# A Mamba mixer in a two-layer trunk: its operand normalized ahead of the transposes, its decay masked by an addition, its convolution read from PSUM

## The chip, the cores and the metric

The kernel runs on one core of a Trainium2 chip. The metric is the device time of one execution in microseconds. A core has five engines with queues of their own: TensorE (PE in the profile; PEld is its weight load), VectorE (DVE), ScalarE (ACT), GpSimd (POOL) and SyncE (SP), which here issues most of the DMAs. Matmuls write to PSUM; all else lies in SBUF or DRAM.

## What is computed

A trunk of two layers on 256 tokens of width 1024, all in 32-bit floats. Each layer is a half-step feed-forward block, a token mixer, an attention into 256 memory tokens, and a second half-step block; each reads an RMS-normalized operand. Layer 0's mixer is a differential attention, layer 1's a Mamba-2 mixer (SSD), which is the part that is changed. Cut to its core:

```python
def rmsnorm(x, w):
    return x * lax.rsqrt(jnp.mean(x * x, axis=-1, keepdims=True) + EPS) * w

# the mixer: u = rmsnorm(h) @ w_in, cut into z (2048), xBC (4096), dt (32)
# xBC = silu(causal_depthwise_conv(xBC, conv_w, conv_b)), cut into x, B, C; 8 groups of 4 heads
# dt = softplus(dt + dt_bias); a = -exp(A_log) * dt; chunks of 128 tokens
a_cs = jnp.cumsum(a, axis=2)
seg = a_cs[..., :, None] - a_cs[..., None, :]
decay = jnp.exp(jnp.where(tril, seg, -jnp.inf))
cb = jnp.einsum("bclgn,bcsgn->bgcls", Cm, Bm)
y_diag = jnp.einsum("bgcls,bgrcls,bcsgrp->bclgrp", cb, decay, x)
# y = y_diag + what the state of the first chunk adds to the second + D_skip * x
# out = rmsnorm by group (y * silu(z)) @ w_out
```

The square root of the mean square is taken by token, so a token's scale can be applied to h ahead of the projection, or to the projection's result behind it. Both are used below.

## The kernel before

**Products.** PE's inputs are split into a rounded high half and the rest (`whi`/`wlo` of a weight, `xh`/`xl` of the operand), and each product is three matmuls (L209 to L211, `mm3`). A weight arrives by a DMA on SP's queue into one of four buffers; a granule of 1024 columns of it is split by a cast on ACT (L180, `whi`) and a subtraction on DVE (L181, `wlo`), two granules ahead of its use (`AHEAD = 2`), into one of four pairs of buffers. For the z projection the subtraction is put on POOL by `eng=nc.gpsimd`; it comes out there for four granules.

**Order.** The program is written by a small pipeline, `Pipe`: `pipe.after(us, f)` puts a piece of work off until PE's estimated time has advanced by `us`, with the delays in the table `T`. A scheduler then settles the order on each engine by a model of its own. Each engine executes its queue in order, so that what stands behind a waiting instruction waits too.

**The mixer** (`ssd`) runs from 800 to 1058 us of the profiled execution, in this order: `zdt` (the first 256 columns of z and the 32 of dt: 48 matmuls), the memory keys `mk` of the layer's later attention, which need nothing of the mixer (four projections in two units, 192 matmuls of 128x256), then four cycles of two groups each: the projections `b`, `c`, `xs` and z, and among them the inner work of the two groups before; then the output product.

- *Operand.* `Norm.turn` transposes h as it is (`xt`, L327) and splits it into `xh`, `xl`. `Norm.square` squares h by token on ACT, and `rpow` gets the scale `rcol` by a power on POOL (L290). As x isn't normalized, the scale is applied behind each product: to dt and z as a scalar by token, and for the convolution, which has tokens along its free dimension, by a row `rr` (`to_row`, L293: two matmuls and a copy on ACT).
- *dt.* `dt_fin` makes dt and a (`av`) with a chain of small operations on DVE and one exponential on ACT (L878 to 899). `sums` (L902) makes the cumulative sums by matmuls, `acs` by token and `acst` by head, writes `acst` to a DRAM scratch `scr` and spreads it from there with partition broadcasts: `E[g, c]`, 128x512 for each of 8 groups and 2 chunks. Four groups are spread at once, the other four later, one by one.
- *Decay.* For each group `decay` takes on POOL the decay to the chunk's end (`dte`, L928, with an exponential on ACT at L930) and E − acs (L933). `decay2` takes the minimum with 0 on DVE (L939) and the exponential on ACT (L940).
- *Convolution.* `conv` scales the projection in PSUM by the row into an SBUF tile `raw` (DVE, L945), and for each of two halves multiplies by the last tap on ACT (L950), adds three taps on DVE (L953) and applies Silu with the bias on ACT (L955). Silu and the exponential lie in different tables of ACT; a change of table shows as `ACT_TABLE_LOAD`.
- *Groups.* `cross` makes C·B (`pcb`, L1009), masks it by the triangle `triu` into `cbm` (DVE, L1011) and multiplies both chunks' E by it (DVE, L1014). `turn_x` transposes x (`tx`, L1020) and makes the products with dt, dte and D on POOL (L1026 to 1030). `inner` makes `pst` and `py`, `state` makes `pof`, adds, multiplies by Silu of z on POOL (L1059), squares on ACT, takes the scale `yrc` on POOL (L290) and applies it on DVE (L1066). `turn_y` transposes y (`ty`, L1073) and splits it for the output product.

```python
            for c in (0, 2):
                proj("a", a["xa_w_kv"][self.l], c * 256, 512, self, "mk", [fin(c), fin(c + 1)])
```

Of the kernel before, what the change touches and what calls it, by code (L numbers as in the profile page):

```python
# [15 lines left out]
P = 128  # L16
S = 256
# [9 lines left out]
         xprobs=5.0, xtp=5.5, xo=3.0, sums=9.5, cross=10.0, cross0=14.5, tx=10.0, tx0=12.0, inner=7.0, state=4.5,  # L27
         ty=9.0, e0=8.0, e1=1.0, e4=33.0, e5=16.5, e6=11.0, dec=2.2)
# [30 lines left out]
def trunk(ctx, tc, a, out):  # L59
# [153 lines left out]
    def proj(kind, src, c0, ncol, norm, name, fins, eng=None):  # L213
# [79 lines left out]
    def to_row(col, dst):  # L293

        ps = small_ps("rrow")
        for t in range(2):
            nc.tensor.matmul(ps[:, t * P:(t + 1) * P], lhsT=col[:, t:t + 1].broadcast_to([P, P]), rhs=ident,
                             start=t == 0, stop=t == 1)
        nc.scalar.copy(dst, ps[:, :S])

    class Norm:
# [3 lines left out]
        def __init__(self, gcol):  # L305
            self.g = gcol
            self.x = []
            self.ss = sm.tile([P, 16], F32, name="nss", tag="nss")
            self.n = 0

        def square(self, c):
# [23 lines left out]
        def add(self, c):  # L335

            def go():
                self.turn(c)
                self.square(c)
            pipe.after(T["turn"], go)  # L340

        def row(self):
            self.rr = sm.tile([P, S], F32, name="rrow", tag="rrow", bufs=2)
            to_row(self.col, self.rr)

    def bc2(row):
        return row.unsqueeze(1).broadcast_to([P, 2, S])
# [380 lines left out]
    class MemKV:  # L728
# [17 lines left out]
        def k_units(self, then=None):  # L746
# [10 lines left out]
            for c in (0, 2):  # L757
# [81 lines left out]
    def ssd(norm, nxt, kv):  # L839
# [8 lines left out]
        dte = const.tile([P, 32], F32, name="dte")  # L848
        E = {}
# [4 lines left out]
        def z0_dt_unit():  # L854
            w, w2 = W(w_in, 0, KT, 0, 256), W(w_in, 0, KT, 6144, 32)

            def run(*gr):
# [10 lines left out]
                def then():  # L868
                    dt_fin([p[:, 256:288] for p in ps])
                    zs0 = v2(slot("zs"))  # L870
                    for t in range(2):
                        nc.scalar.activation(zs0[:, t, :], ps[t][:, 0:256], AF.Copy, scale=norm.col[:, t:t + 1])
                    held.append(zs0)
                pipe.after(T["gate"], then)
                pipe.after(T["gate"] + 2.0, norm.row)
            units.append(([Gran(k, n, (w, 0, 256), (w2, 0, 32)) for k, n in ((0, 3), (3, 3), (6, 2))], run))

        def dt_fin(pd):  # L878
            xd = const.tile(d32, F32, name="dtx")
            for t in range(2):  # L880
                v.scalar_tensor_tensor(xd[:, t, :], pd[t], norm.col[:, t:t + 1], dtb, op0=ALU.mult, op1=ALU.add)
# [20 lines left out]
        def sums():  # L902

# [22 lines left out]
        def decay(g):  # L926
# [4 lines left out]
            for c in range(2):  # L931
                e = E[g, c]
                nc.gpsimd.tensor_tensor(e, e, acs[:, c, hs].unsqueeze(2).broadcast_to([P, 4, P]), op=ALU.subtract)  # L933
# [317 lines left out]
```

## Time and profile before

| | us |
|---|---|
| runs, median of 3 | 1337.58 (1336.15 to 1338.41) |
| profiled execution | 1336.94 |
| its span | 1335.1 |
| layer 1's mixer in it | 800.1 to 1058.0 |

The span reaches from the first to the last instruction that the profiler recorded; the execution's own time is 1.8 us longer. An engine's busy time leaves out the time in which it waits or only issues DMAs. In the rows of a window stand its bounds and length, the busy time of each engine with its number of instructions, then the clock that was granted to TensorE (1.00 is full), the DMA engines' share and GB/s. In a timeline a row is a start, a duration, the engine, the line and what it writes and reads, with the idle time ahead of it and what ended that in brackets. The slices of the page (40 equal parts, tenths of busy time) show the mixer as the stretch from the 25th slice on where DVE is fullest and POOL works at all:

```profile
DVE  5555457876566555555556456998988675655553
POOL 1000002200000000000000001444423000000000
```

### The profile page before, as it was taken

To read this page: it belongs to the slowest core of one execution; us is meant where nothing else is said; L and a number is where in the kernel's file an instruction comes from. 1 tells how busy PE (TensorE), PEld (TensorE's weight loads), DVE (VectorE), ACT (ScalarE), POOL (GpSimd) and SP (SyncE) were. 2 spreads that over 40 slices of the span, in tenths; PEclk is the share of its full clock that TensorE was granted. 3 is DMA by queue.
4 is the path that set the end of the run, shared out by engine and by line. 5 is a ranking of instruction groups with operands and counts; after the bars stand their busy time and mean duration, and the time that the engine had idled before them with its cause. 6 is when DMAs were issued, how large, how long until landed. Compare 5 with 4: busy or idle time off the path is not lost.

```text
span 1335.1 us, 17775 instructions
## 1 busy us (share of the span) xinstructions
PE 1301.0 (97%) x6991; PEld 1115.8 (84%) x6991; DVE 842.7 (63%) x1207; ACT 714.2 (53%) x1125; POOL 115.0 (9%) x109
## 2 busy tenths in 40 slices
PE   6999999999999999999999999988999999999997
PEld 5888888778988888888888889988897898888886
DVE  5555457876566555555556456998988675655553
ACT  5445544676455544444445445767756564644432
POOL 1000002200000000000000001444423000000000
PEclk9999999999999999999999999999999999999999
DMA  8564555334535554655555546634544544555551
GB/s 268 191 218 155 195 203 177 126 130 152 190 128 177 173 194 133 221 193 201 189 187 175 191 149 231 225 118 135 169 145 156 177 158 151 193 177 174 204 174 48
DMA packets 133254, 232.01 MB, mean 174 GB/s; under 512 B 5273, under 2 KB 32066, under 8 KB 133170
## 3 DMA queue, kind: packets, MB, share of 16 engines
q1 hardware_dynamic: 132496, 229.56, 52.2%
q0 software_dynamic: 368, 0.98, 0.3%
q8 instruction: 55, 0.90, 0.3%
q10 hardware_dynamic: 306, 0.33, 0.1%
q14 instruction: 29, 0.24, 0.1%
HBM read 229.77 MB, written 1.08 MB: 173 GB/s over the span
## 4 chain that ended last, share of the span: by engine, by line
PE 85%; DVE 9%; ACT 2%; POOL 2%; DMA 1%; issue 1%; POOLq 0%; DVEq 0%; ACTq 0%; SPq 0%
PE out L211 7%; PE out L210 7%; PE out L209 7%; PE gate L210 6%; PE gate L211 6%; PE gate L209 5%; PE up L209 5%; PE up L210 5%; PE up L211 5%; DVE wlo L181 2%; PE fin L209 1%; PE fin L211 1%; PE fin L210 1%; PE htp L551 1%; DVE xs L953 1%; PE mv L209 1%
## 5 line engine op out<-in xcount | busy, mean ns | idle before, releaser
L181 DVE TENSOR_TENSOR wlo<-w,whi 128x1024 fp32r<-128x1024 f32 (+1 forms) x440 | 522.9, 1194 | 408.6 <-ACT whi L180 407.6
L180 ACT CAST whi<-w 128x1024 fp32r<-128x1024 f32 (+1 forms) x444 | 446.8, 1012 | 461.4 <-PE out L211 142.5
L210 PE MATMUL gate<-wlo,xh 128*128 128x512 f32 x320 | 126.1, 394 | 2.2 <-DVE wlo L181 2.2
L209 PE MATMUL gate<-whi,xh 128*128 128x512 f32 x320 | 127.6, 400 | 0.0
L211 PE MATMUL gate<-whi,xl 128*128 128x512 f32 x320 | 125.8, 393 | 0.0
L209 PE MATMUL up<-whi,xh 128*128 128x512 f32 x320 | 124.6, 389 | 0.0
L211 PE MATMUL up<-whi,xl 128*128 128x512 f32 x320 | 124.6, 389 | 0.0
L210 PE MATMUL up<-wlo,xh 128*128 128x512 f32 x320 | 124.6, 389 | 0.0
L209 PE MATMUL out<-whi,hid_hi 128*128 128x512 f32 x264 | 103.6, 393 | 0.0
L211 PE MATMUL out<-whi,hid_lo 128*128 128x512 f32 x264 | 102.9, 390 | 0.0
L210 PE MATMUL out<-wlo,hid_hi 128*128 128x512 f32 x264 | 102.8, 390 | 0.0
L210 PEld LDWEIGHTS gate<-wlo,xh 128*128 128x128 f32 x320 | 60.9, 190 | 14.9 <-DVE wlo L181 3.0
L211 PEld LDWEIGHTS gate<-whi,xl 128*128 128x128 f32 x320 | 60.8, 190 | 12.6
L209 PEld LDWEIGHTS gate<-whi,xh 128*128 128x128 f32 x320 | 60.9, 191 | 12.0
L209 PEld LDWEIGHTS up<-whi,xh 128*128 128x128 f32 x320 | 60.1, 188 | 12.4
L211 PEld LDWEIGHTS up<-whi,xl 128*128 128x128 f32 x320 | 60.1, 188 | 12.4
L210 PEld LDWEIGHTS up<-wlo,xh 128*128 128x128 f32 x320 | 60.1, 188 | 12.4
L290 POOL TENSOR_TENSOR rcol<-msq,neghalf 128x2 f32<-128x2 f32 x8 | 5.6, 700 | 700.4 <-DVE msq L288 700.4
L211 PEld LDWEIGHTS out<-whi,hid_lo 128*128 128x128 f32 x264 | 49.6, 188 | 10.4
L210 PEld LDWEIGHTS out<-wlo,hid_hi 128*128 128x128 f32 x264 | 49.6, 188 | 10.0
L209 PEld LDWEIGHTS out<-whi,hid_hi 128*128 128x128 f32 x264 | 49.6, 188 | 10.0
L209 PE MATMUL fin<-whi,hid_hi 128*128 128x512 f32 (+1 forms) x110 | 38.3, 348 | 0.0
(352 smaller groups left out, 2777.9 us busy)
## 6 DMA issues: line engine op xcount, KB each, us to landing
w<-in_ffn_w_up_dram SPq DMA_DIRECT2D x40, 1024.0 KB, 5.0
w<-in_ffn_w_down_dram SPq DMA_DIRECT2D x40, 1024.0 KB, 5.1
w<-in_ffn_w_gate_dram SPq DMA_DIRECT2D x38, 1024.0 KB, 5.0
w<-in_ssd_w_in_dram SPq DMA_DIRECT2D x24, 1024.0 KB, 5.2
w<-in_xa_w_kv_dram SPq DMA_DIRECT2D x16, 1024.0 KB, 4.9
w<-in_da_w_in_dram SPq DMA_DIRECT2D x12, 1024.0 KB, 5.0
w<-in_xa_w_q_dram SPq DMA_DIRECT2D x8, 1024.0 KB, 5.0
w<-in_xa_w_o_dram SPq DMA_DIRECT2D x8, 1024.0 KB, 5.0
```

What stands on the lines that cost most here:

```text
L180: nc.scalar.copy(hv, src)
L181: self.eng.tensor_tensor(self.lo[:, :, o:o + n], src, hv.bitcast(F32), op=ALU.subtract)
L209: nc.tensor.matmul(o, lhsT=lh, rhs=rh, start=start, stop=False)
L210: nc.tensor.matmul(o, lhsT=lh, rhs=rl, start=False, stop=False)
L211: nc.tensor.matmul(o, lhsT=ll, rhs=rh, start=False, stop=stop)
L290: nc.gpsimd.tensor_tensor(c[:, :n], m[:, :n], neghalf[:, :n], op=ALU.pow)
L551: nc.tensor.transpose(tp[:, j, t * P:(t + 1) * P], us[t][:, (i + j) * P:(i + j + 1) * P], ident)
L953: v.scalar_tensor_tensor(o[:, j, d:], raw[:, j, :S - d], tap(k), o[:, j, d:], op0=ALU.mult, op1=ALU.add)
```

## The change

The norm ahead of layer 1's mixer is made with `first=True`: it squares h first, and when the scale is there ACT writes four tiles `hn` = h × scale, from which the transposes are made. The operand is thus normalized, the row `rr` is gone, and z, dt and the convolution use their products as they are. The key unit is cut in two: one unit of two projections ahead of `zdt`, one behind it. What followed `zdt` after a delay (`gate`) now follows at once.

The mask is a tile `later` (0 where the row may see the column, −1e30 where not), made once in `sums`. POOL adds it behind E − acs; the minimum and the triangle are gone, and E is multiplied by `pcb` in PSUM directly. The convolution reads its taps from PSUM. The scaling of y goes from DVE to ACT, and z's low halves from POOL to DVE. The delays in `T` are new.

```diff
 T = dict(gate=5.5, hid=3.0, turn=1.3, row=5.0, rot=5.5, probs=(1.0, 4.0, 7.0, 10.0), tp=6.0, heads=3.0, otp=5.0,
-         xprobs=5.0, xtp=5.5, xo=3.0, sums=9.5, cross=10.0, cross0=14.5, tx=10.0, tx0=12.0, inner=7.0, state=4.5,
-         ty=9.0, e0=8.0, e1=1.0, e4=33.0, e5=16.5, e6=11.0, dec=2.2)
+         xprobs=5.0, xtp=5.5, xo=3.0, sums=7.0, cross=9.0, cross0=13.0, tx=9.0, tx0=11.0, inner=8.0, state=6.0,
+         ty=13.0, e0=8.0, e1=5.0, e4=33.0, e5=16.5, e6=11.0, dec=6.5, first=7.0)
...
-                        xh, xl = norm.x[kt]
+                        xh, xl = pipe.need(norm.x, kt)
...
                 self.col = rpow(s[:, 0:2], 1.0 / D, 2, "rcol")
+                if self.first:
+                    self.src = [[slot("hn") for _ in range(2)] for _ in range(2)]
+                    for i in range(2):
+                        for t in range(2):
+                            nc.scalar.activation(self.src[t][i], h[t][i], AF.Copy, scale=self.col[:, t:t + 1])
+                        pipe.after(T["first"] + 1.5 * i, lambda i=i: self.turn(i))
...
-                        nc.tensor.transpose(ps[:, j, t * P:(t + 1) * P], h[t][c][:, f:f + P], ident)
+                        nc.tensor.transpose(ps[:, j, t * P:(t + 1) * P], self.src[t][c][:, f:f + P], ident)
...
-                        nc.scalar.activation(zs0[:, t, :], ps[t][:, 0:256], AF.Copy, scale=norm.col[:, t:t + 1])
+                        nc.scalar.copy(zs0[:, t, :], ps[t][:, 0:256])
                     held.append(zs0)
-                pipe.after(T["gate"], then)
-                pipe.after(T["gate"] + 2.0, norm.row)
+                then()
...
-                v.scalar_tensor_tensor(xd[:, t, :], pd[t], norm.col[:, t:t + 1], dtb, op0=ALU.mult, op1=ALU.add)
+                v.tensor_tensor(xd[:, t, :], pd[t], dtb, op=ALU.add)
...
         def sums():
+            v.tensor_scalar(later, triu, 1e30, 1e30, op0=ALU.mult, op1=ALU.subtract)
...
                 nc.gpsimd.tensor_tensor(e, e, acs[:, c, hs].unsqueeze(2).broadcast_to([P, 4, P]), op=ALU.subtract)
+                nc.gpsimd.tensor_tensor(e, e, later.unsqueeze(1).broadcast_to([P, 4, P]), op=ALU.add)
             pipe.after(T["dec"], lambda: decay2(g))

         def decay2(g):
             for c in range(2):
-                e = E[g, c]
-                v.tensor_scalar(e, e, 0.0, None, op0=ALU.min)
-                nc.scalar.activation(e, e, AF.Exp)
+                nc.scalar.activation(E[g, c], E[g, c], AF.Exp)

         def conv(ps, ch, name):
-            raw = v2(work("raw"))
-            v.tensor_tensor(raw, ps, bc2(norm.rr), op=ALU.mult)
...
-                nc.scalar.activation(o[:, j, :], raw[:, j, :], AF.Copy, scale=tap(3))
+                nc.scalar.activation(o[:, j, :], ps[:, j, :], AF.Copy, scale=tap(3))
                 for k in (2, 1, 0):
                     d = 3 - k
-                    v.scalar_tensor_tensor(o[:, j, d:], raw[:, j, :S - d], tap(k), o[:, j, d:],
+                    v.scalar_tensor_tensor(o[:, j, d:], ps[:, j, :S - d], tap(k), o[:, j, d:],
                                            op0=ALU.mult, op1=ALU.add)
...
-                    nc.scalar.activation(zs[:, t, :], ps[t], AF.Silu, scale=norm.col[:, t:t + 1])
+                    nc.scalar.activation(zs[:, t, :], ps[t], AF.Silu)
...
-                cbm = work("cbm", S).rearrange("p (c l) -> p c l", c=2)
-                v.tensor_tensor(cbm, pcb[:, 0:2, :], triu.unsqueeze(1).broadcast_to([P, 2, P]), op=ALU.mult)
-                s["cbm"] = cbm
                 for c in range(2):
-                    v.tensor_tensor(E[g, c], E[g, c], cbm[:, c, :].unsqueeze(1).broadcast_to([P, 4, P]), op=ALU.mult)
+                    v.tensor_tensor(E[g, c], E[g, c], pcb[:, c, :].unsqueeze(1).broadcast_to([P, 4, P]), op=ALU.mult)
+                s["cbm"] = True
...
-                    v.tensor_scalar(y[:, t, :], y[:, t, :], rc[:, t:t + 1], None, op0=ALU.mult)
+                    nc.scalar.activation(y[:, t, :], y[:, t, :], AF.Copy, scale=rc[:, t:t + 1])
...
+        kv.k_units(cs=(0,))
         z0_dt_unit()
-        kv.k_units()
+        kv.k_units(cs=(2,))
...
-                proj("b", w_in, 256, 256, norm, "z", [lambda ps, f=fz[1]: f([ps[:, t, :] for t in range(2)])], eng=nc.gpsimd)
+                proj("b", w_in, 256, 256, norm, "z", [lambda ps, f=fz[1]: f([ps[:, t, :] for t in range(2)])])
...
-    nx = Norm(gains("mix_norm", l))
+    nx = Norm(gains("mix_norm", l), first=l == 1)
```

How the order of the engines' work changes is shown at three places. On PE, the sums' products among the memory keys (a row is a line, an operation, what it writes and reads, and its shape), before:

```order
L210 MATMUL mk<-ml,whi 128x256
L211 MATMUL mk<-mh,wlo 128x256
L905 MATMUL acs<-av,cst 128x64
L908 MATMUL acst<-cst,av 32x128 x2
L209 MATMUL mk<-mh,whi 128x256
```

and with the change:

```order
L209 MATMUL mk<-mh,whi 128x256
L210 MATMUL mk<-ml,whi 128x256
L902 MATMUL acs<-av,cst 128x64
L905 MATMUL acst<-cst,av 32x128 x2
L211 MATMUL mk<-mh,wlo 128x256
```

Before, 132 key matmuls lie between zdt and these rows, and 60 between them and b; now 77 and 19. The 96 others are ahead of zdt, with the transposes from `hn` among them: 72 ahead of the first eight, 12 between these and the second eight, 12 behind.

On POOL, the decay of the third and fourth group (the number of an E tells its tile, two for each group). Before:

```order
L928 TENSOR_TENSOR dte_130<-E_6995,acs_128 128x4
L933 TENSOR_TENSOR E_6995<-E_6995,acs_128 128x512
L933 TENSOR_TENSOR E_6997<-E_6997,acs_128 128x512
L928 TENSOR_TENSOR dte_130<-E_6999,acs_128 128x4
L933 TENSOR_TENSOR E_6999<-E_6999,acs_128 128x512
```

and with the change, where the fourth group's dte is the last row:

```order
L925 TENSOR_TENSOR dte_130<-E_7033,acs_128 128x4
L930 TENSOR_TENSOR E_7033<-E_7033,acs_128 128x512
L930 TENSOR_TENSOR E_7035<-E_7035,acs_128 128x512
L931 TENSOR_TENSOR E_7033<-E_7033,later_131 128x512
L931 TENSOR_TENSOR E_7035<-E_7035,later_131 128x512
L925 TENSOR_TENSOR dte_130<-E_7037,acs_128 128x4
```

Twelve large operations now lie ahead of the fourth dte, where there were six.

On ACT, the exponentials of the third and fourth group, around the convolutions of b and c in the first cycle. Before (whi_7213 and whi_7257 are granules of the weights of xs):

```order
L940 ACTIVATE E_6999<-E_6999 128x512
L940 ACTIVATE E_7001<-E_7001 128x512
L950 ACTIVATE b_7167<-raw_7165,cols2_115 128x256 x2
L180 CAST whi_7213<-w_7215 128x1024
L180 CAST whi_7257<-w_7181 128x1024
L955 ACT_TABLE_LOAD
```

and with the change (whi_7274 is the second granule of the second xs projection):

```order
L927 ACTIVATE dte_130<-dte_130 128x4
L936 ACTIVATE E_7033<-E_7033 128x512
L936 ACTIVATE E_7035<-E_7035 128x512
L949 ACT_TABLE_LOAD
L949 ACTIVATE b_7148<-b_7148,cols1_114 128x256
L944 ACTIVATE b_7148<-b_7083,cols2_115 128x256
L944 ACTIVATE c_7228<-c_7159,cols2_115 128x256
L180 CAST whi_7274<-w_7192 128x1024
L180 CAST whi_7317<-w_7319 128x1024
L936 ACT_TABLE_LOAD
L936 ACTIVATE E_7037<-E_7037 128x512
L949 ACT_TABLE_LOAD
```

The first of these rows is the exponential of the fourth group's dte. The casts whi_7274 and whi_7317 stand behind it, and behind a table load, and the two halves of a convolution are apart, with loads of tables between Silu and the exponentials.

More of the change, by code (lines that the diff above doesn't have):

```diff
@@ L291, in rpow, with __init__ @@
         return c
[L293 to L299, printed above, removed]
     class Norm:
-        def __init__(self, gcol):
+        def __init__(self, gcol, first=False):
             self.g = gcol
+            self.first = first
+            self.src = h
             self.x = []
@@ L337, in go @@
             def go():
-                self.turn(c)
+                if not self.first:
+                    self.turn(c)
                 self.square(c)
             pipe.after(T["turn"], go)
[L342 to L347, printed above, removed]
     def v2(t, j=2):
@@ L744, in prep, with k_units @@
                 self.x.append((xh, xl))
-        def k_units(self, then=None):
+        def k_units(self, then=None, cs=(0, 2)):
             def fin(c):
@@ L756, in fin @@
                 return run
-            for c in (0, 2):
+            for c in cs:
                 proj("a", a["xa_w_kv"][self.l], c * 256, 512, self, "mk", [fin(c), fin(c + 1)])
@@ L848, in ssd @@
         dte = const.tile([P, 32], F32, name="dte")
+        later = const.tile([P, P], F32, name="later")
         E = {}
@@ L1090, in ssd @@
             if i == 0:
-                proj("b", w_in, 256, 256, norm, "z", [lambda ps, f=fz[1]: f([ps[:, t, :] for t in range(2)])], eng=nc.gpsimd)
+                proj("b", w_in, 256, 256, norm, "z", [lambda ps, f=fz[1]: f([ps[:, t, :] for t in range(2)])])
             else:
                 wide([(w_in, 512 * i, 512)], norm, "z",
-                     lambda ps, fz=fz: [f([p[:, j * 256:(j + 1) * 256] for p in ps]) for j, f in enumerate(fz)], eng=nc.gpsimd)
+                     lambda ps, fz=fz: [f([p[:, j * 256:(j + 1) * 256] for p in ps]) for j, f in enumerate(fz)])
         out_b(a["ssd_w_out"][0], 16, yt, upd(1.0, nxt), both=True)
```

## The prediction

> **What bounds the kernel now.** I read the page's table of engines first, then the windows of layer 1's mixer, then what TensorE (PE) waited for there, then the timelines of the engines it waited for, and the order in which each engine now issues its work.
>
> ```profile
> span 1335.1 us, 17775 instructions
> PE 1301.0 (97%) x6991; PEld 1115.8 (84%) x6991; DVE 842.7 (63%) x1207; ACT 714.2 (53%) x1125; POOL 115.0 (9%) x109
> ```
>
> PE is busy 97% of the span, so only two things can change the time: matmuls that go or come, and PE's waits. The change touches layer 1's mixer alone. Its stages, by windows (length, then busy time of PE, PEld, DVE, ACT, POOL, granted clock, DMA):
>
> ```profile
> 800.10:832.00 31.90, 31.87 (x260) 31.37 (x259) 20.60 (x39) 18.81 (x29) 1.66 (x3) 1.00 0.66 225
> 832.00:862.90 30.90, 29.80 (x247) 29.40 (x246) 27.74 (x40) 22.20 (x38) 12.40 (x12) 1.00 0.70 223
> 862.90:913.50 50.60, 45.91 (x322) 42.94 (x321) 47.65 (x77) 36.47 (x66) 22.50 (x18) 0.93 0.46 146
> 913.50:962.80 49.30, 43.42 (x308) 39.83 (x307) 43.51 (x66) 37.02 (x65) 22.50 (x20) 1.00 0.45 143
> 962.80:1006.30 43.50, 42.81 (x307) 39.80 (x306) 38.20 (x61) 25.58 (x51) 14.73 (x11) 1.00 0.43 146
> 1006.30:1058.00 51.70, 51.20 (x250) 42.70 (x249) 36.67 (x50) 29.77 (x53) 8.21 (x7) 1.00 0.49 163
> ```
>
> The rows are: dt and memory keys, the four cycles (b, c, xs, z), and the output product. Length less PE's busy time is 0.0, 1.1, 4.7, 5.9, 0.7 and 0.5 us. DVE is busy 88 to 94% of each cycle, so in the second and third PE waits for work that stands behind others on DVE:
>
> ```profile
> PE ty L1073 <- DVE y L1066: 4.7, 1, 4.7
> PE pof L1054 <- ACT state L1040: 3.1, 1, 3.1
> PE tx L1020 <- ACT xs L955: 1.4, 2, 1.0
> PE z L210 <- DVE wlo L181: 1.4, 1, 1.4
> PE xs L211 <- DVE wlo L181: 1.1, 2, 0.7
> ```
>
> The 4.7 us wait costs twice. In the five microseconds behind it the granted clock was 0.53, so about 2.3 us of work were lost there too:
>
> ```profile
> 897.00:902.00 5.00, 4.67 (x17) 4.07 (x18) 4.41 (x12) 3.06 (x9) 0.99 (x2) 0.53 0.42 118
> ```
>
> **All that the change can win** is thus 12.9 us of idle time, 2.3 us of slow clock, and small holes between matmuls, about 2 us by the records' spacing (an estimate): 17 us, of which 1.6 lie in the first cycle, 7.3 in the second, 7.3 in the third and the rest behind.
>
> **The change, part by part.** First what DVE sheds, from its groups in the mixer:
>
> ```profile
> L1014 DVE TENSOR_TENSOR E<-E,cbm 128x512 f32<-128x512 f32 x16 | 15.8, 1018 | 0.1
> L939 DVE TENSOR_SCALAR E<-E 128x512 f32<-128x512 f32 x16 | 14.2, 927 | 6.5 <-POOL E L933 6.5
> L1066 DVE TENSOR_SCALAR y<-y,yrc 128x256 f32<-128x256 f32 x16 | 6.7, 461 | 5.0 <-POOL yrc L290 5.0
> L1011 DVE TENSOR_TENSOR cbm<-pcb,cst 128x256 f32<-128x256 f32 x8 | 3.3, 410 | 0.0
> L945 DVE TENSOR_TENSOR raw<-xs,rrow 128x512 f32<-128x512 f32 x8 | 5.4, 678 | 0.0
> L181 POOL TENSOR_TENSOR wlo<-w,whi 128x1024 fp32r<-128x1024 f32 x4 | 9.6, 2405 | 33.4 <-ACT whi L180 33.4
> ```
>
> The minimum goes (14.2), the triangle (3.3), the normalization of the convolutions' inputs (16 × 0.678 = 10.8) and the scaling of y (6.7): 35.0 us. Four low halves of z's weights come back from POOL: 4 × 1.2 = 4.9. Two groups should get quicker, because of what they share with POOL. Operations between two SBUF tiles have a long tail, those with an operand in PSUM have none:
>
> ```profile
> L953 DVE SCALAR_TENSOR_TENSOR xs<-raw,cols,xs x48: 466/473/2002, 855.7 to 1003.8; 128x255 f32<-128x255 f32 x16, 128x254 f32<-128x254 f32 x16, 128x253 f32<-128x253 f32 x16
> L945 DVE TENSOR_TENSOR raw<-xs,rrow x8: 673/676/683, 854.4 to 999.4; 128x512 f32<-128x512 f32 x8
> L283 DVE SCALAR_TENSOR_TENSOR y_lo<-ty,cols,y_hi x16: 468/475/485, 904.9 to 1037.9; 128x256 fp32r<-128x256 f32 x16
> ```
>
> (shortest, median, longest, ns). The 96 taps would take their median, about 5 us less in all; the 16 multiplications of E by PSUM 0.68 in place of 1.018, 5.4 less. Together DVE sheds some 40 of its 214 us. A tap from PSUM I price as a tap from SBUF: y_lo, which reads PSUM in the same form, takes 475 against 473 ns. The Trainium skill speaks against this part: "VectorE: DVE Perf Modes", section "Rules for kernel authors", says to copy out of PSUM first where many operations follow. By that advice the removed raw copy would pay for itself; y_lo's row here says that there is nothing to be won by it, and the sum is the same without this sentence.
>
> ACT gets 16 scalings of y, priced as its squares of y (0.41, 6.6 us), and four of h, priced as its squares of h (0.62, 2.5), loses the row's copy (0.4), and by its new order has 26 table loads in the mixer where it had 16:
>
> ```profile
> L1063 ACT ACTIVATE junk<-y 128x256 f32<-128x256 f32 x16 | 6.5, 409 | 8.6 <-POOL y L1059 8.6
> L314 ACT ACTIVATE sq<-h 128x512 f32<-128x512 f32 x6 | 3.7, 620 | 0.0
> L955 ACT ACT_TABLE_LOAD x7 | 9.0, 1283 | 10.6 <-DVE xs L953 5.3 <-DVE b L953 3.8 <-DVE c L953 1.4
> ```
>
> Ten more of 1.283 us are 12.8. ACT so goes from 36.5 and 37.0 in the second and third cycle (four or three loads and four scalings more each) to about 43, against 43 to 46 of PE work: no longer a free engine. The skill's "ScalarE: Activation LUTs", section on what a table load costs, puts a switch at 2.66 us, with a drain; by that the ten would cost 26.6 us. The trace has the next operation 1.29 us behind a load's start (846.62, then 847.91), so 1.283 stands.
>
> ```profile
> L933 POOL TENSOR_TENSOR E<-E,acs 128x512 f32<-128x512 f32 x16 | 18.5, 1176 | 0.6
> L290 POOL TENSOR_TENSOR rcol<-msq,neghalf 128x2 f32<-128x2 f32 x2 | 1.4, 696 | 217.5 <-DVE msq L288 217.5
> L358 DVE SCALAR_TENSOR_TENSOR h<-out,h 128x512 f32<-128x512 f32 x2 | 1.4, 690 | 0.6 <-PE out L211 0.6
> ```
>
> POOL gets 16 additions of the mask as large as its subtractions, which take 1.18 us on average and 1.04 undisturbed (the pair at 840.13, below): 16.6 to 18.9 more, less the 9.6 above.
>
> PE loses the row's two products, under half a microsecond. The normalization now stands between the end of the last out product and the transposes. From the last matmul that is h's update (0.69 twice), the squares, the sums, the power on POOL (0.70) and four scalings, in all about 6 us; 72 key matmuls (8.7 us at the 0.12 us of the second window's 247 in 29.80) lie over it. I cost it at nothing; without the cover it would be those 6 us.
>
> **The new wait.** The keys that cover the normalization no longer cover what follows dt. From dtx to av it takes 9.85 us, then the sums, a trip through DRAM and the spread to E:
>
> ```profile
> 808.20 0.41 DVE L881 SCALAR_TENSOR_TENSOR dtx<-zdt,rcol,vec 128x32 f32<-128x32 f32 x2
> 817.83 0.23 DVE L899 SCALAR_TENSOR_TENSOR av<-dt,nega 128x64 f32<-128x64 f32 x1
> 823.86 0.33 PE L905 MATMUL acs<-av,cst 128*128 128x64 f32 x2
> 830.96 0.62 POOL L928 TENSOR_TENSOR dte<-E,acs 128x4 f32<-128x4 f32 x1 [27.16 <-DMA E<-scr]
> 836.63 3.08 POOL L933 TENSOR_TENSOR E<-E,acs 128x512 f32<-128x512 f32 x2
> 840.13 2.09 POOL L933 TENSOR_TENSOR E<-E,acs 128x512 f32<-128x512 f32 x2
> 840.20 1.66 ACT L940 ACTIVATE E<-E 128x512 f32<-128x512 f32 x3
> 844.55 1.99 ACT L180 CAST whi<-w 128x1024 fp32r<-128x1024 f32 x2
> 846.62 1.28 ACT L955 ACT_TABLE_LOAD   x1
> 847.91 0.91 ACT L955 ACTIVATE b<-b,cols 128x256 f32<-128x256 f32 x2
> ```
>
> I count from the first zdt matmul. The 48 of zdt end at 6.4 (0.133 each), the acs product follows 77 key matmuls later, at 15.6; av is there at 16.5, a wait of **0.9 us**. From acs to POOL's start it takes 7.1 us: about 24, where b's matmuls, begun at 19.5, are just ending; before, POOL began one microsecond ahead of b. Ahead of its fourth dte POOL now has twelve operations of 1.04 and three small ones, 14.1 us: that dte ends at 38.3, or up to 41.4 with three weight splits of DVE beside it (one cost POOL 1.0 us at 836.63).
>
> On ACT's new order stand behind this dte two exponentials, a table load, a Silu and two taps, and only then the cast whi of the second xs product's second part: 0.2 + 1.2 + 1.3 + 0.5 + 1.0 + 1.0 = 5.2 us, done at 43.5 to 46.6. PE wants it at about 39.7, then its wlo, behind DVE's taps. **PE waits 5 to 8 us, say 6.7.** ACT goes on late, with two more pairs of loads before it reaches the last Silu of xs, which the tx transposes need: another 2 to 5 us, say 3.6. With 0.9 us of old holes that is 11.2 in the first cycle against 1.6: **+9.6**; and behind a wait of over 4.7 us I expect the slow clock again, **+1.6**, less than the 2.3 above as 256-wide matmuls follow.
>
> In the later cycles DVE's relief does what it should, but an exponential that waits for POOL's mask additions (some 3 to 4 us) and the scaling of y behind POOL's power now hold up ACT. I leave 4.0 of 7.3 in the second (−3.3), 3.9 of 7.3 in the third (−3.4), and −1.0 behind. Start: 0.9 − 0.4 = +0.5. Sum: 0.5 + 9.6 + 1.6 − 3.3 − 3.4 − 1.0 = +4.0. The profiled run took 1336.94 us for a span of 1335.1, 0.6 under the runs' median of 1337.58: **1341.0**.
>
> **The rivals.**
> - *DVE's relief decides, faster (0.35).* ACT's place in the order harms nobody if POOL's fourth dte is done by about 33: subtractions at less than 1.04 or E landing earlier. Then the first cycle keeps its 1.6, or loses 2: 0.5 + 0.4 − 3.3 − 3.4 − 1.0 = −6.8, 1330; if the waits of the second and third cycle go wholly, 7 us more, 1323. For it: PE's two longest waits stood behind DVE. Against it: POOL's undisturbed 1.04.
> - *The two cancel (0.20).* A first-cycle wait of 7 to 8 us in all gives 1336 to 1339.
> - *ACT becomes the bound (within the slower cases, 0.13).* If ACT's 97 to 100% of PE's time in the middle cycles leaves no room, nothing is won there, and each of the 10 loads on the path is up to 1.28: +11.7 of the first terms and start, with −1 behind, and 0 to 4 of loads: 1348 to 1352.
> - *The keys don't cover the normalization:* another 2 to 4 us on any of these, if the whi casts of the keys go ahead of the squares on ACT. POOL's and DVE's share of that chain is short; I give it no chance of its own.
> - *PSUM held longer by taps:* conv's banks are wanted again 10 us or more behind their last reader by the order; dismissed.
>
> **How the numbers follow.** The likeliest, the wait for the fourth dte, has 0.32 with 1341 (1338.5 to 1347); ACT as the bound 0.13; cancelled 0.20; faster 0.35. A measurement of this kernel tells about 0.2%, 2.7 us, from no change. Faster 0.35, same 0.20, slower 0.45. The range, with the low end inside the faster case and the high end at ACT's: 1324 to 1350.
>
> **What would show it.** A PE wait of 5 us or more in the second xs product for wlo or whi, at some 40 us from the first zdt matmul; POOL's fourth dte ending at 38 or later; 26 table loads in the mixer; no wait at zdt; DVE's groups of taps at 473 ns without a tail. A fourth dte at 33, or the cast ahead of it in time, would make me wrong towards faster; ACT over 45 us busy in the middle cycles towards slower.

## The result, and the profile after

The changed kernel takes **1344.96 us** (median of 4 runs, 1343.45 to 1346.02), the kernel before 1337.99 in the same series: a ratio of 1.0053, 95% interval 1.0041 to 1.0065. It is slower by 7.0 us, on the side that was forecast and inside the range (1324 to 1350), 4 us above the number.

The page of the changed kernel, its span and its engines:

```profile
span 1341.7 us, 17757 instructions
PE 1300.8 (97%) x6987; PEld 1116.7 (83%) x6987; DVE 810.5 (60%) x1156; ACT 734.2 (55%) x1154; POOL 123.7 (9%) x121
```

PE's busy time over the whole span is the same to 0.2 us, so the span is longer by waiting: in the mixer's windows PE stood 19.2 us, where it stood 12.9 before. DVE's busy time fell by 32 us, ACT's rose by 20, POOL's by 9. The windows of the changed kernel, in the columns of those of before, with bounds at the same places of the program:

```profile
798.60:831.10 32.50, 32.19 (x263) 31.75 (x262) 21.49 (x46) 24.54 (x41) 0.70 (x1) 1.00 0.65 217
831.10:872.20 41.10, 33.07 (x252) 32.58 (x251) 20.63 (x31) 26.47 (x42) 20.67 (x20) 0.88 0.52 163
872.20:924.20 52.00, 44.24 (x316) 40.56 (x315) 39.48 (x60) 40.72 (x72) 27.00 (x23) 1.00 0.46 143
924.20:971.00 46.80, 43.69 (x304) 40.57 (x303) 34.98 (x53) 39.70 (x69) 23.78 (x20) 0.96 0.49 157
971.00:1013.70 42.70, 42.70 (x310) 40.05 (x309) 34.89 (x53) 30.43 (x60) 11.07 (x11) 1.00 0.45 155
1013.70:1064.60 50.90, 50.90 (x250) 42.82 (x250) 31.90 (x43) 29.21 (x54) 7.47 (x7) 1.00 0.48 160
```

From first b matmul to first b matmul the cycles take 41.1, 52.0, 46.8 and 42.7 us where they took 30.9, 50.6, 49.3 and 43.6: +10.2, +1.4, −2.5, −0.9; the output product wins 0.8. Counted from the last matmul of the `out` product ahead of the mixer (799.85 before, 798.35 now), b starts 0.7 us later. That is 8.1 us in the mixer. The spans differ by 6.6 alone, as the part ahead of the mixer ended 1.5 us earlier in this execution; over all profiled executions here it ended between 798.35 and 802.40. The slow clock is there too, 0.88 in the first cycle: 0.50 and 0.54 in the two stretches of 5 us from 856.1 to 866.1, behind the wait in xs. What PE waited for in the mixer, after the change:

```profile
PE xs L209 <- ACT whi L180: 6.5, 1, 6.5
PE pcb L1003 <- ACT c L949: 6.3, 3, 3.5
PE tx L1012 <- ACT xs L949: 2.9, 1, 2.9
PE z L209 <- DVE E L1005: 1.6, 1, 1.6
PE xs L211 <- DVE wlo L181: 1.5, 1, 1.5
```

The old waits for DVE's y and ACT's state are gone. In their place stands first the cast in the second xs product. Rows of POOL's timeline of the changed kernel show how late it starts (the first group's dte), then the third group and the fourth group's dte:

```profile
836.72 0.20 POOL L925 TENSOR_TENSOR dte<-E,acs 128x4 f32<-128x4 f32 x1 [34.43 <-DMA E<-scr]
848.25 0.20 POOL L925 TENSOR_TENSOR dte<-E,acs 128x4 f32<-128x4 f32 x1
848.53 2.04 POOL L930 TENSOR_TENSOR E<-E,acs 128x512 f32<-128x512 f32 x2
850.53 2.51 POOL L931 TENSOR_TENSOR E<-E,later 128x512 f32<-128x512 f32 x2
852.99 0.20 POOL L925 TENSOR_TENSOR dte<-E,acs 128x4 f32<-128x4 f32 x1
```

and ACT's, behind it:

```profile
853.23 0.20 ACT L927 ACTIVATE dte<-dte 128x4 f32<-128x4 f32 x1 [3.49 <-POOL dte L925]
853.34 1.13 ACT L936 ACTIVATE E<-E 128x512 f32<-128x512 f32 x2
854.47 1.28 ACT L949 ACT_TABLE_LOAD   x1
855.77 0.51 ACT L949 ACTIVATE b<-b,cols 128x256 f32<-128x256 f32 x1
856.18 0.45 ACT L944 ACTIVATE b<-b,cols 128x256 f32<-128x256 f32 x1
856.54 0.46 ACT L944 ACTIVATE c<-c,cols 128x256 f32<-128x256 f32 x1
856.89 1.99 ACT L180 CAST whi<-w 128x1024 fp32r<-128x1024 f32 x2
```

POOL starts 5.6 us behind b's first matmul, not 1.0 ahead of it; its fourth dte is done 41.4 us behind the first zdt matmul; ACT stands 3.5 us for it and then has 3.7 us of other work ahead of a cast that PE already waits for.

### The profile page after: what moved, and what is told of

It reads as the page before. It is cut to its first block, busy times and chain, and to the rows that moved or that the text cites. A ratio compares the mean times of both kernels' runs of the same rounds, so it can differ in the third digit from the quotient of the medians.

```text
span 1341.7 us, 17757 instructions
## 1 busy us (share of the span) xinstructions
PE 1300.8 (97%) x6987; PEld 1116.7 (83%) x6987; DVE 810.5 (60%) x1156; ACT 734.2 (55%) x1154; POOL 123.7 (9%) x121
## 4 chain that ended last, share of the span: by engine, by line
PE 88%; DVE 4%; POOL 3%; issue 2%; ACT 1%; DMA 1%; POOLq 0%; DVEq 0%; ACTq 0%; SPq 0%
PE out L211 7%; PE out L209 7%; PE out L210 7%; PE gate L210 5%; PE gate L211 5%; PE up L211 5%; PE up L210 5%; PE up L209 5%; PE gate L209 5%; PE fin L209 1%; PE fin L210 1%; PE fin L211 1%; PE htp L546 1%; PE mv L209 1%; PE mk L209 1%
## 5 line engine op out<-in xcount | busy, mean ns | idle before, releaser
L181 DVE TENSOR_TENSOR wlo<-w,whi 128x1024 fp32r<-128x1024 f32 (+2 forms) x444 | 532.7, 1206 | 424.2 <-ACT whi L180 423.0
L180 ACT CAST whi<-w 128x1024 fp32r<-128x1024 f32 (+2 forms) x444 | 446.7, 1012 | 454.9 <-PE out L211 136.3
L209 PE MATMUL xs<-xh,whi 128*128 128x256 f32 x128 | 38.6, 301 | 6.5 <-ACT whi L180 6.5
```

Of the source, the lines that this page charges most:

```text
L180: nc.scalar.copy(hv, src)
L181: self.eng.tensor_tensor(self.lo[:, :, o:o + n], src, hv.bitcast(F32), op=ALU.subtract)
L209: nc.tensor.matmul(o, lhsT=lh, rhs=rh, start=start, stop=False)
```

## The experiments

Eleven runs, each of them the changed kernel or the kernel before with an edit. The table has the time, its ratio to the kernel before with the 95% interval, and the four cycles, from first b matmul to first b matmul of the profiled run (us). The kernel before ran beside each series, with medians of 1337.0 to 1338.0; the ratio is to the one of the same series.

| run | us | ratio | 1st | 2nd | 3rd | 4th |
|---|---|---|---|---|---|---|
| before | 1337.99 | 1 | 30.9 | 50.6 | 49.3 | 43.6 |
| the change | 1344.96 | 1.0053 (1.0041 to 1.0065) | 41.1 | 52.0 | 46.8 | 42.7 |
| spread_late | 1344.59 | 1.0063 (1.0045 to 1.0081) | 37.3 | 47.7 | 48.6 | 46.0 |
| yscale_dve | 1343.55 | 1.0051 (1.0036 to 1.0066) | 40.1 | 51.5 | 46.9 | 43.2 |
| keys_back | 1347.00 | 1.0072 (1.0056 to 1.0089) | 41.8 | 51.1 | 42.2 | 42.4 |
| b_mask | 1349.89 | 1.0093 (1.0078 to 1.0108) | 41.8 | 51.0 | 50.8 | 42.6 |
| b_keys | 1341.93 | 1.0038 (1.0024 to 1.0052) | 39.4 | 46.3 | 49.2 | 45.3 |
| min_back | 1332.08 | 0.9963 (0.9950 to 0.9976) | 33.9 | 48.2 | 44.6 | 43.1 |
| min_back_keys_back | 1336.46 | 0.9992 (0.9982 to 1.0002) | 34.6 | 48.5 | 42.3 | 42.9 |
| stt_dve | 1334.75 | 0.9977 (0.9968 to 0.9987) | 31.2 | 54.6 | 41.9 | 42.9 |
| sub_min_dve | 1334.55 | 0.9973 (0.9964 to 0.9983) | 32.7 | 54.7 | 43.1 | 42.5 |
| min_back_yscale | 1334.64 | 0.9980 (0.9971 to 0.9989) | 32.6 | 51.0 | 46.8 | 42.9 |
| min_back_raw | 1343.83 | 1.0048 (1.0031 to 1.0064) | 36.0 | 49.7 | 52.3 | 42.2 |

### Is the cast's place on ACT what costs the first cycle?

spread_late sends the spreads of two groups later, so that ACT's order has the casts ahead of them.

```diff
-                pipe.after(T["e0"] + T["e1"] * g if g < 4 else T["e6"], lambda: decay(g))
-            for g in range(4):
+                pipe.after(T["e0"] + T["e1"] * g if g < 2 else T["e0"] if g < 4 else T["e6"], lambda: decay(g))
+            for g in range(2):
                 spread(g)
+            pipe.after(20.0, lambda: spread(2))
+            pipe.after(26.0, lambda: spread(3))
```

> The changed kernel, with the spreads of the third and fourth group sent 20 and 26 us after the sums (of PE's estimated time) and not at once; nothing else is edited. The order on ACT then has the casts for the second xs product ahead of these two groups' dte and exponentials, and 40 table loads in the program for 32. Queue theory (the first cycle's loss is the cast that stands on ACT behind POOL's fourth dte): that cast is done near 852 where the changed kernel had it at 858, so the waits of PE in the second xs product fall from 8.3 us to 1 to 3, and the first cycle, 41.1 us long now, gets 5 to 8 shorter; with the loads and the later groups moved into the second cycle the whole is 2 to 8 us faster than the changed kernel, 1337 to 1343. Load theory (ACT's table loads themselves are the price): 8 loads more, 10 us, so 1350 or more.

The cast came at 851.07, in time, and PE's wait for it (6.5 us) was gone; the wait for the low half, 1.4, stayed (two rows of ACT's timeline):

```profile
847.06 0.63 ACT L938 ACTIVATE E<-E 128x512 f32<-128x512 f32 x1 [2.62 <-POOL E L933]
851.07 1.04 ACT L180 CAST whi<-w 128x1024 fp32r<-128x1024 f32 x1
```

The first cycle got 3.8 us shorter, less than expected: in it z now waited 2.7 us for a low half and 0.6 for a cast. The second won 4.3, the third and fourth lost 5.1, with 34 loads in the mixer for 26. The median didn't change beyond the runs' scatter (1342.1 to 1347.8). So the wait for the cast does come from its place in the order, but moving it this way wins nothing that can be told.

### Is ACT's added work the price of the later cycles?

yscale_dve puts the 16 scalings of y back on DVE.

```diff
-                    nc.scalar.activation(y[:, t, :], y[:, t, :], AF.Copy, scale=rc[:, t:t + 1])
+                    v.tensor_scalar(y[:, t, :], y[:, t, :], rc[:, t:t + 1], None, op0=ALU.mult)
```

> The changed kernel, with the scaling of y back on DVE. ACT's order in the first cycle is the same row by row. Queue theory: the wait of 6.5 us in the first cycle stays within half a microsecond; in the later cycles ACT no longer waits 8.2 us for POOL's power in front of the scalings, so the second and third cycle together get 2 to 5 us shorter: 1340 to 1343. Load theory (ACT's busy time bounds these cycles): 7.6 us of work leave ACT and the second and third cycle get at least 4 shorter, in proportion to it. If DVE is the bound again: nothing, or slower.

The first cycle's wait is 6.3. The second and third cycle got 0.4 us shorter together, so taking 7.6 us of work off ACT wins next to nothing there. DVE got 5.7 us more by it, which could have hidden a gain; this run alone can't tell. PE's wait for pcb behind Silu of c stayed at 6.0.

### The keys, or the mask?

keys_back calls the key unit whole behind zdt again; b_mask and b_keys put one part of the change alone into the kernel before; min_back takes the mask alone out of the change, and min_back_keys_back both.

```diff
# keys_back
-        kv.k_units(cs=(0,))
         z0_dt_unit()
-        kv.k_units(cs=(2,))
+        kv.k_units()
# min_back
-                nc.gpsimd.tensor_tensor(e, e, later.unsqueeze(1).broadcast_to([P, 4, P]), op=ALU.add)
...
-                nc.scalar.activation(E[g, c], E[g, c], AF.Exp)
...
+                v.tensor_scalar(e, e, 0.0, None, op0=ALU.min)
+                nc.scalar.activation(e, e, AF.Exp)
...
+                v.tensor_tensor(cbm, pcb[:, 0:2, :], triu.unsqueeze(1).broadcast_to([P, 2, P]), op=ALU.mult)
...
-                    v.tensor_tensor(E[g, c], E[g, c], pcb[:, c, :].unsqueeze(1).broadcast_to([P, 4, P]), op=ALU.mult)
...
+                    v.tensor_tensor(E[g, c], E[g, c], cbm[:, c, :].unsqueeze(1).broadcast_to([P, 4, P]), op=ALU.mult)
```

> The changed kernel, with both units of keys behind zdt, as before the change. Queue theory: nothing covers the normalization, so PE waits 5 to 7 us ahead of the first transposes; but E is spread 11.5 us earlier against b, POOL's fourth dte ends ahead of the second xs product, and the first cycle loses 1 to 3 us where it lost 10. Sum 2 to 6 us under the changed kernel: 1339 to 1343. Rival (the loss comes from POOL's additions wherever they lie): first cycle unchanged, and the time is the changed kernel's plus the wait of 5 to 7: 1350.

> The kernel before with the mask alone: the added tile on POOL, no minimum, no triangle, E multiplied by pcb in PSUM. DVE sheds 17.5 us and what the multiplications of E gain, 5; the order on PE is that of before. Queue theory: POOL starts one microsecond ahead of b as before, but its fourth dte ends near 848 and the fourth group's exponentials, behind which stand the casts for xs, near 851: PE waits 5 to 9 us in the first cycle, and the later cycles win 2 to 6: 1338 to 1344. Relief theory (what DVE sheds decides): 4 to 8 us faster than before, 1330 to 1334.

Both came out against my theory of the time, that POOL's late start behind the moved keys makes the loss. With the keys back, POOL started 0.9 us ahead of b's first matmul, and the first cycle was still 41.8 us long; a wait of 4.4 us for the normalization came on top. ACT's order now has other casts behind the same exponentials. In rows of ACT's timeline of keys_back it waits twice more than 3 us for POOL ahead of the cast that PE then waits for in xs (2.7 us; another held c for 2.2):

```profile
855.36 0.21 ACT L927 ACTIVATE dte<-dte 128x4 f32<-128x4 f32 x1 [3.59 <-POOL dte L925]
859.84 0.63 ACT L936 ACTIVATE E<-E 128x512 f32<-128x512 f32 x1 [3.23 <-POOL E L931]
860.74 1.03 ACT L180 CAST whi<-w 128x1024 fp32r<-128x1024 f32 x1
```

The mask alone, put into the kernel before, is worse than the whole change: +12 us, 10.9 of them in the first cycle, though DVE sheds the minimum and the triangle there and the keys haven't moved. PE's waits in that run show the old ones (4.7 and 2.6) kept, and the casts added. The added ones in xs, 8.0 us, are within the 5 to 9 that I expected; the win in the later cycles, by which I had 1338 to 1344, did not come:

```profile
PE xs L209 <- ACT whi L180: 5.6, 2, 4.9
PE ty L1072 <- DVE y L1065: 4.7, 1, 4.7
PE pof L1053 <- ACT state L1039: 2.6, 1, 2.6
PE xs L211 <- DVE wlo L181: 2.4, 2, 1.8
```

So I changed the theory: it is the mask's additions on POOL, wherever the keys lie, and the next three runs were to settle it. (b_mask has the old table `T`, so the new delays aren't needed for the loss.)

> The changed kernel, with the mask undone alone: minimum and triangle on DVE again, no addition on POOL; all the rest of the change stays. Mask theory (16 additions of 1.29 us on POOL make the first cycle's loss, wherever the keys lie): POOL's fourth dte ends near 845 where it was 853, the cast behind it is in time, and the first cycle, 41.1 us, falls to 31 to 35; DVE, with 17.5 us of work back, costs the later cycles 0 to 4. Sum 4 to 9 us under the changed kernel: 1336 to 1341. Cover theory (the keys taken from behind zdt make it): the first cycle stays at 38 or more and the time at 1343 or more.

> The kernel before with the key move alone: one unit of keys ahead of zdt, one behind it. The operand isn't normalized ahead here, so nothing is covered by it. Mask theory: E comes 6 us later against b, but POOL's four groups of subtractions take only 10 us, so the first cycle loses 1 to 4 us: 1338 to 1342. Cover theory: the casts stand behind POOL's late dte as with the whole change, and the first cycle loses 8 or more: 1345.

> The changed kernel with both undone, mask and key move. Mask theory: the first cycle is that of the kernel before within 2 us (31 to 33); PE waits the 4.5 us for the normalization that the run with the keys back showed; the later cycles win 0 to 4 from what is left of DVE's relief: 1336 to 1342, no better than with the mask undone alone. Were the key move a loss, this one would be the faster of the two.

min_back settles it. Without the mask the change is **faster than the kernel before, 1332.08 us, ratio 0.9963**, and 12.9 us faster than with it, more than I had expected. POOL's start, its third group and the fourth dte in min_back, and the cast behind them:

```profile
838.43 0.20 POOL L924 TENSOR_TENSOR dte<-E,acs 128x4 f32<-128x4 f32 x1 [34.82 <-PE b L211]
843.23 0.38 POOL L924 TENSOR_TENSOR dte<-E,acs 128x4 f32<-128x4 f32 x1
843.69 3.08 POOL L929 TENSOR_TENSOR E<-E,acs 128x512 f32<-128x512 f32 x2
846.73 0.38 POOL L924 TENSOR_TENSOR dte<-E,acs 128x4 f32<-128x4 f32 x1
```

```profile
847.14 0.20 ACT L926 ACTIVATE dte<-dte 128x4 f32<-128x4 f32 x1 [0.60 <-POOL dte L924]
847.25 0.61 ACT L936 ACTIVATE E<-E 128x512 f32<-128x512 f32 x1
847.77 1.03 ACT L180 CAST whi<-w 128x1024 fp32r<-128x1024 f32 x1
```

POOL starts as late here as with the mask, 6.0 us behind b's first matmul (832.45) for 5.6. But counted from that matmul the fourth dte took 14.7 us, with the mask 22.1 (831.14 to 853.19), and the cast ended at 16.4 for about 26.8 (the first of the pair at 856.89). The first cycle fell by 7.2 us, the second by 3.7, the third by 2.2. PE's longest waits in the mixer are now small:

```profile
PE tx L1014 <- ACT xs L949: 3.0, 3, 1.8
PE z L210 <- DVE wlo L181: 2.2, 2, 1.9
PE z L209 <- ACT bn L998: 1.5, 1, 1.5
PE pcb L1003 <- ACT c L949: 1.3, 2, 0.7
```

Four runs thus cross the two choices (the change, keys_back, min_back, min_back_keys_back). With the mask on POOL the first cycle takes 41.1 us when POOL starts late and 41.8 when it starts ahead of b; without it 33.9 (late) and 34.6 (ahead).

The key move alone (b_keys) costs the kernel before 4 us, 8.4 in the first cycle less 4.2 in the second; there dt's later steps still wait for the delays `gate` and `sums` of the old table, so POOL starts 11.7 us behind b. With the normalization ahead it is a gain: min_back is 4.4 us faster than min_back_keys_back, where PE waits 4.4 us for `hn`, and their first cycles are alike (33.9 and 34.6).

### Other ways to make the mask, and what the rest of the change brings

stt_dve makes the subtraction and the mask in one operation by head on DVE; sub_min_dve the subtraction and the minimum, with the triangle as before. Both leave POOL only the dte. In each it was 64 operations, not 128 as I wrote (8 groups, 2 chunks, 4 heads).

```diff
# stt_dve
-                nc.gpsimd.tensor_tensor(e, e, acs[:, c, hs].unsqueeze(2).broadcast_to([P, 4, P]), op=ALU.subtract)
-                nc.gpsimd.tensor_tensor(e, e, later.unsqueeze(1).broadcast_to([P, 4, P]), op=ALU.add)
+                for r in range(4):
+                    v.scalar_tensor_tensor(e[:, r, :], e[:, r, :], acs[:, c, 4 * g + r:4 * g + r + 1], later,
+                                           op0=ALU.subtract, op1=ALU.add)
# sub_min_dve (the triangle comes back as in min_back)
-                nc.gpsimd.tensor_tensor(e, e, acs[:, c, hs].unsqueeze(2).broadcast_to([P, 4, P]), op=ALU.subtract)
-                nc.gpsimd.tensor_tensor(e, e, later.unsqueeze(1).broadcast_to([P, 4, P]), op=ALU.add)
...
+                for r in range(4):
+                    v.tensor_scalar(e[:, r, :], e[:, r, :], acs[:, c, 4 * g + r:4 * g + r + 1], 0.0,
+                                    op0=ALU.subtract, op1=ALU.min)
```

> The changed kernel, with subtraction and mask in one operation on DVE: E minus acs plus the mask as scalar_tensor_tensor of 128x128 by head, 128 of some 0.2 to 0.27 us (26 to 34 us on DVE, 39 us off POOL); POOL keeps the dte alone. Mask theory: the dte come at once, the cast is not held, the first cycle falls to 31 to 35; DVE's 183 us in the mixer become about 213, as before the change, so the later cycles win little. 1334 to 1341. If DVE's added work stands ahead of the low halves of the weights instead, the first cycle stays above 36 and the time near the changed kernel's.

> The changed kernel with minimum and triangle, and the subtraction of acs taken from POOL into the minimum: one tensor_scalar of 128x128 by head on DVE (subtract, then min), 128 of some 0.15 to 0.2 us (19 to 26) for the 16 of some 0.4 to 0.9 with the mask undone; POOL sheds 17 us. If what POOL does ahead of ACT's exponentials is the price, the first cycle falls from 33.9 to 31 to 33 and the whole to 1328 to 1332. If the order on ACT (38 table loads in the program for 30) counts more: 1333 to 1337, with tx waiting for ACT in the second cycle.

In both the first cycle falls to 31 to 33 us: with nothing on POOL ahead of them the exponentials hold no cast. The change that is 7 us slower than the kernel before with the mask added on POOL is thus 2.9 us faster than it when DVE adds the same mask. Both runs then lose 4.1 us in the second cycle against the kernel before. tx waits there for ACT's Silu of xs (6.5 and 5.5 us in the mixer), with 32 loads of tables in the mixer for min_back's 24. That the loads make those waits is not shown: min_back_keys_back has 20 loads, and tx waits 6.1 us. And waiting is not all of it. PE's idle time in that cycle is 2.7 us (stt_dve) and 0.3 us (sub_min_dve) above the kernel before's; the other 1.4 and 3.8 are matmuls that took longer, at a granted clock of 0.91 and 0.88 for 0.93.

min_back_yscale and min_back_raw undo one more part each.

```diff
# min_back_raw (beside the edit of min_back)
+            raw = v2(work("raw"))
+            v.tensor_copy(raw, ps)
...
-                nc.scalar.activation(o[:, j, :], ps[:, j, :], AF.Copy, scale=tap(3))
+                nc.scalar.activation(o[:, j, :], raw[:, j, :], AF.Copy, scale=tap(3))
...
-                    v.scalar_tensor_tensor(o[:, j, d:], ps[:, j, :S - d], tap(k), o[:, j, d:],
+                    v.scalar_tensor_tensor(o[:, j, d:], raw[:, j, :S - d], tap(k), o[:, j, d:],
```

> The changed kernel with the mask undone and the scaling of y on DVE again. If what is left of PE's waits is ACT's (tx behind Silu of xs, 3.0 us; z behind bn, 1.5; pcb, 1.3), the 7.6 us that leave ACT win 1 to 3 us on the run with the mask undone: 1329 to 1331. If DVE, now with 24 us of work back, bounds the later cycles again: 1334 to 1337. In between: ACT's waits for POOL, which this doesn't touch, are what counts, and the time is within 1.5 us of 1332.

> The changed kernel with the mask undone, and the convolution's input copied from PSUM to SBUF on DVE ahead of its taps (16 copies of 128x512, a plain copy in place of the multiplication by the row that the kernel before had). If taps cost the same from PSUM, as the trace says, this adds 11 us of DVE work and brings back the tail that taps between SBUF tiles had beside POOL: 1 to 5 us slower than 1332, with median taps again at 0.47 us. If many operations on PSUM pay for a copy, as the skill advises, the taps get quicker by more than the copy, and the time is under 1332.

With y scaled on DVE the median is 2.6 us above min_back's; the two ratios' intervals just overlap. The move to ACT is a small gain, if it is one. With the copy back it is **11.8 us slower** than min_back, more than twice what I had expected. The taps of xs in the two runs, min_back first:

```profile
L947 DVE SCALAR_TENSOR_TENSOR xs<-xs,cols x48: 463/474/485, 858.2 to 998.6; 128x255 f32<-128x255 f32 x16, 128x254 f32<-128x254 f32 x16, 128x253 f32<-128x253 f32 x16
```

```profile
L949 DVE SCALAR_TENSOR_TENSOR xs<-raw,cols,xs x48: 468/478/1503, 858.8 to 1007.6; 128x255 f32<-128x255 f32 x16, 128x254 f32<-128x254 f32 x16, 128x253 f32<-128x253 f32 x16
L941 DVE COPY raw<-xs x8: 677/682/684, 856.2 to 1002.4; 128x512 f32<-128x512 f32 x8
```

From PSUM a tap costs the same at the median and nothing in the tail; all taps of b, c and xs took 45.2 us for 51.8, and the copies 10.9. For work on a matmul's output, the Trainium skill gives the choice to accept PSUM's rate or to copy out of PSUM first where many operations follow ("VectorE: DVE Perf Modes", "Rules for kernel authors"); the copy loses here by these numbers. PE's waits for low halves went from 2.2 us to 11.6 (z 6.3, xs 3.5, b 1.8), so DVE's relief here was on the path. Not all of the 11.8 us need be the taps' and the copies': the order on ACT changed too, with 30 loads in the mixer for 24.

## Why the prediction was right or wrong

**Right, and shown:** the sign, and the mechanism of the first cycle. The wait stood where it was put, in the second xs product for the cast whi behind POOL's fourth dte and a table load. It was forecast at 6.7 us and took 6.5, with 1.5 more for the low half. The fourth dte ended at 41.4 us, the upper end of 38.3 to 41.4, and the cast behind it was late by as much. The slow clock came (0.88). spread_late took that wait away by the order alone.

Term by term, from the windows of the two profiled executions (us; a cycle's waits are its length less PE's busy time):

| term | forecast | measured |
|---|---|---|
| start | +0.5 | +0.7 |
| first cycle, waits | +9.6 | +6.9 |
| first cycle, matmuls that take longer | +1.6 | +3.2 |
| second cycle | −3.3 | +1.4 |
| third cycle | −3.4 | −2.5 |
| behind | −1.0 | −1.7 |
| sum | +4.0 | +8.1 |

**Right in part by luck:** the size of the first cycle. Its +10.2 is near the +11.2 that was forecast, but the 3.6 us for tx behind the last Silu of xs did not come: PE waited for no transpose in this cycle, and 8.0 us in all for the 11.2 that the forecast added up. The slow clock cost about twice its 1.6 (some 0.6 of the 3.2 are five matmuls more in the window).

**Right in size:** 26 loads; ACT near 40 us in the middle cycles (43 forecast); the taps 45.3 us for 50.6, 5.3 less where 5 was forecast, without a tail; E × pcb 0.68 (10.7 us for 15.8); DVE shed 31 us in the mixer where I had 40, in part as its weight splits took 1.38 us on average for 1.31. The keys covered the normalization: no wait ahead of zdt. PE waited 0.3 us for dt where 0.9 was forecast.

**Wrong in a term:** "I leave 4.0 of 7.3 in the second (−3.3)". The second cycle lost 1.4 us. That step alone is 4.7 us off; the third was −2.5 for −3.4. PE's old waits there did go, as forecast, but pcb waited 5 us and tx 3 in their place, behind Silu of c and of xs on ACT. What ACT waited for in cycles two to four, in the changed kernel and then in min_back:

```profile
ACT y L1058 <- POOL yrc L290: 6.1, 3, 4.7
ACT junk L1055 <- POOL y L1051: 5.1, 4, 3.8
ACT E L936 <- POOL E L931: 3.2, 1, 3.2
```

```profile
ACT y L1060 <- POOL yrc L290: 2.8, 3, 1.9
ACT E L936 <- DVE E L935: 2.6, 2, 1.5
ACT junk L1057 <- POOL y L1053: 2.3, 5, 0.7
```

I had named two of these waits (the exponential, the scaling) and not the third, the squares of y behind POOL's product with Silu of z, which stands behind the same additions. ACT stood 14.4 us for POOL by these rows; without the mask 5.1, and 2.6 for DVE. I also priced an addition at 1.04, and undisturbed it takes 1.29:

```profile
L930 POOL TENSOR_TENSOR E<-E,acs x16: 1038/1040/2026, 837.0 to 950.4; 128x512 f32<-128x512 f32 x16
L931 POOL TENSOR_TENSOR E<-E,later x16: 1262/1293/2295, 838.1 to 951.6; 128x512 f32<-128x512 f32 x16
```

**Wrong in a reason:** the text put two grounds for the late dte beside each other, and the cover first: "The keys that cover the normalization no longer cover what follows dt", and then the twelve operations ahead of it. By the runs the loss is the mask's: alone it costs 12 us, and taken away it returns 12.9, of them 7.2 in the first cycle. What then remains over the kernel before in that cycle, 3.0 us, is about as long with the keys back (34.6); but the waits in it are others there (c for a low half and tx, in place of z for a low half), so that the keys have no part in it isn't shown. The late start of POOL, read from the change's order, did come; what the additions do where POOL starts early was not asked.

**The rivals.** DVE's relief is real: with the mask out it gives 1332, where that rival had 1330. It was given 0.35 on the condition that POOL's fourth dte came in time, and that condition failed through the mask. ACT as the bound was not it: ACT was busy 40.7 of 52.0 us and 39.7 of 46.8 in the middle cycles, and taking 7.6 us of work off it moved the time by 1.4 us, within the scatter. PSUM held longer by taps: nothing of it in PE's waits. But z's 1.6 us behind E × pcb would fit a bank of PSUM held longer by what now reads pcb there; that it was the bank is not shown.

**Open:** why the scheduler puts casts behind exponentials that come late. The casts follow POOL's additions in three orders (the change, keys_back, b_mask), which would fit a model that prices these additions too low, but no run tested that. Also open are the second cycle's loss in stt_dve and sub_min_dve, with the slower clock in it, and what the normalization ahead, the low halves moved to DVE and the new delays are worth one by one; no run undid them alone.

## What to carry to other kernels

Work moved off a busy engine is gained only if the queue of the engine that receives it is not on the path: DVE did shed 32 us here, but 16 additions on POOL stood ahead of ACT's exponentials, and these ahead of the casts whose weights PE needs next. When an in-order engine gets a wait, list what stands behind it, above all the work of the next stage. Test the parts of a mixed change one by one: all but the mask were together a gain of 5 to 6 us here, hidden by it.

## What I had not expected of the hardware

A POOL addition of a mask with its 128 columns repeated four times takes 1.29 us where the subtraction of a column of scalars on the same tile takes 1.04. And a tap from PSUM is not only as quick as one from SBUF; it has no tail beside POOL (longest of 48 for xs in min_back 0.485 us, of 48 from SBUF 1.5, in the kernel before 2.0). In the timelines of min_back_raw and the kernel before, every stretch of taps that averages over 0.52 us each lies over 1 us or more of POOL's operations; in min_back taps lie over them too and take no longer. With the copies saved, and the order that came with it, this was worth 11.8 us of 1344. A cause that fits stands in the Trainium skill: "SBUF — State Buffer", section "Who interferes with whom", says that VectorE and GpSimd share a port pair, and that a VectorE operation with at most one SBUF input, outside its two-port modes, does not contend with GpSimd. The rows agree (0.485 us for 1.5 and 2.0).
